# Pinning VectorE's order around the delta rule chain in a hybrid decoder step

## The chip, the cores and the metric

The kernel runs on one core of one Trainium2 chip, as one launch. The metric is the device time of that launch in microseconds (us). TensorE (PE) multiplies matrices, VectorE (DVE) and ScalarE (ACT) work element by element, GpSimd (POOL) does small things and issues transfers, and SyncE (SP) issues transfers. Each engine works through its own list of instructions; semaphores order the lists among each other.

## The reference

One decoder layer for 1024 prompt tokens and 8 sample tokens: a SwiGLU block, a mixer, a second SwiGLU block, each closed by a layer norm. The mixer runs an RG-LRU branch and a gated delta rule branch side by side. The change lies in the delta rule. For each of 8 heads and each chunk of tokens it computes, with a state S of 128 x 128:

```
def step(S, inp):
    qd, kt, ui, wi, ai, gl = inp
    v_new = ui - wi @ S
    o = qd @ S + ai @ v_new
    S = S * exp(gl) + kt.T @ v_new
    return S, o
...
o = o * rsqrt(mean(square(o), -1) + RMS_EPS) * gdn_norm_w
out_b = o * silu(z)
merged = sigmoid(gate_a) * out_a + sigmoid(gate_b) * out_b
return merged @ w_o
```

## The kernel before

All activations lie transposed, channels on the 128 partitions and the 1032 tokens along the free dimension, in three chunks of 344 (`TC`). Matmuls are done in three passes on operands split into a high and a low part (`mm3_steps`, L172). The kernel has three stages: the first SwiGLU up to some 740 us, the mixer up to some 1775 us, the second SwiGLU.

In the mixer two programs are woven together. The first is the delta rule of one head, the generator `gdn`: a preparation (norms, decays, the inverse of a triangular matrix), and then a chain of 8 chunks of 128 tokens. The second is the `stream`, the projections of the mixer's input with all that follows them: keys, queries and values of the next head, the RG-LRU (`rgx`, `rg`), the gates (`gate_b`, `gate_a`). Each `yield` of `gdn` names a weight from the table `W`; times a rate of some 2.1 it gives the number of steps of the stream (three matmuls each) that are issued before `gdn` goes on. The rate spreads the stream evenly over the heads.

The chain, per chunk c, in the program's order:
- p1 (from chunk 1 on): `K` and `Q` times the state `St` into a PSUM bank of the tag `sq` (two banks). VectorE makes r of it (L1103), ScalarE makes `to`. Then `yield W["s1"]`.
- p2: the inverse `U` times r. VectorE scales it by `cs` to v2 (L1110). Then `yield W["s2"]`.
- p3: `KT` and `AT` times v2. VectorE brings the state forward (`St`, L1115) and sums the chunk's output into `O`, which is the tile `vn` (L1116). ScalarE sums the output's squares into `os`. Then `yield W["s3"]`.

The generator `tail(j)` closes the outputs of half a head, four chunks. VectorE adds up (`os`), GpSimd takes the power -1/2 (`os<-os,NHALF`), and after a yield VectorE scales the outputs by these roots (L1087, `vn<-vn,os`, 128 x 512). Then TensorE transposes them (`trs`, L935) and VectorE multiplies them into the gate's tile `ACC`. The first half's tail starts at the end of chunk 3, its scaling stands in the program behind the output sum of chunk 4, and its rest comes after chunk 5. The second half's tail follows the last chunk.

Of the stream, one line matters below: `gate_b` closes each chunk of its projection with a VectorE multiply (L1143, `ACC<-lnq,ACC`) of ScalarE's tanh `lnq` with the gate. `rI<-rI,s` is an RG-LRU step (L1222), `s<-pre,conv_w,s` a step of a convolution (L801).

What sets the order: a compiler's list scheduler makes each engine's list ahead of time. By its own forecast of when operands are there, it takes of the instructions that are ready the earliest one of the program. `tc.keep_in_program_order(x)` (here `pin`) ties x behind the one instruction that the program gave x's engine just before it: x does not come ahead of that one in the list. It makes no semaphore and no wait for that one's end. In the chain the first matmul of each step is pinned in TensorE's list. The stream's matmuls are not, and on VectorE nothing in `gdn` is. Lines that are a helper's (L91 `act`, L94 `tt`, L97 `stt`, L929 `mms`) stand for many operations, so the rows below are read by their tiles.

Of the kernel before, what the change touches and what calls it, by code (L numbers as in the profile page):

```python
# [12 lines left out]
OP = mybir.AluOpType  # L13
# [46 lines left out]
def _build(ctx, tc, A):  # L60
    nc = tc.nc
    V, S, G, PE = nc.vector, nc.scalar, nc.gpsimd, nc.tensor
# [24 lines left out]
    def psum(tag):  # L87
        return ps.tile([128, 512], F32, name="ps_" + tag, tag=tag, bufs=PSB[tag])

    def act(out, in_, f, **kw):  # L90
        return S.activation(out, in_, f, **kw)  # L91

    def tt(out, a, b, op, eng=None):
        return (eng or V).tensor_tensor(out, a, b, op=op)  # L94

    def stt(out, a, s, b, op0, op1):
        return V.scalar_tensor_tensor(out, a, s, b, op0=op0, op1=op1)  # L97

    def bc(ap, shape):
        return ap.to_broadcast(shape)  # L100
# [579 lines left out]
    def mixer(mc):  # L680
# [74 lines left out]
        with pool("mix") as mp:  # L755
            B4 = [128, 4, 128]
# [10 lines left out]
            def blk(tag):  # L767
                return mp.tile([128, 128], F32, name=tag, tag=tag)

            def small(tag):  # L770
                return mp.tile([128, 8], F32, name=tag, tag=tag, bufs=2)
# [4 lines left out]
            def ck(x, c):  # L776
                return x[:, c * 128:(c + 1) * 128]
# [146 lines left out]
            def pin(ins):  # L924
                tc.keep_in_program_order(ins)

            def mms(p, pairs, pinned=True):
                for i, (a, b) in enumerate(pairs):
                    x = PE.matmul(ck(p, i), a, b, start=True, stop=True)  # L929
                    if i == 0 and pinned:  # L930
                        pin(x)

            def trs(p, ins):
                for i, a in enumerate(ins):
                    x = PE.transpose(ck(p, i), a, IDT)  # L935
                    if i == 0:
                        pin(x)

            def gdn(h):
                K, Q, v = KQV[h]  # L940
                C4 = [range(4 * j, 4 * j + 4) for j in range(2)]
                J = [slice(4 * j, 4 * j + 4) for j in range(2)]
                k2s, cs, nh, qe = small("k2s"), small("cs"), small("nh"), small("qe")
# [16 lines left out]
                for j in range(2):  # L960
                    pd = psum("g")
                    for i in range(2):
                        x = PE.matmul(pd, SLR, gu[j][i].rearrange("p c j -> p (c j)"), start=(i == 0), stop=(i == 1))
# [115 lines left out]
                O = VN  # L1079
                os_ = small("os")  # L1080

                def tail(j):
                    o = os_[:, J[j]]
                    stt(o, o, 1.0 / 128, qe[:, J[j]], OP.mult, OP.add)
                    tt(o, o, NHALF[:, :4], OP.pow, G)
                    yield W["ta"]
                    tt(O[:, J[j], :], O[:, J[j], :], bc(o.unsqueeze(2), B4), OP.mult)  # L1087
                    yield W["tb"]
                    yield ("need", ("B", h))
                    pt = psum("g")  # L1090
                    trs(pt, [O[:, c, :] for c in C4[j]])
                    js = slice(512 * j, 512 * j + 512)
                    stt(ACC[:, h, js], pt, NW, ZT[h][:, js], OP.mult, OP.mult)
                    yield W["tc"]

                St = blk("St")
                for c in range(CH):
                    r = VN[:, c, :]
                    if c > 0:
                        p1 = psum("sq")  # L1100
                        mms(p1, [(ck(K, c), St), (ck(Q, c), St)])
                        r = blk("r")
                        stt(r, p1[:, :128], NE[:, c, h:h + 1], VN[:, c, :], OP.mult, OP.add)  # L1103
                        to = blk("to")
                        act(to, p1[:, 128:256], AF.Copy, scale=EX[:, 0, c, h:h + 1])
                        yield W["s1"]
                    p2 = psum("sq")
                    mms(p2, [(U[:, c, :], r)])
                    v2 = blk("v2")
                    V.tensor_scalar(v2, p2[:, :128], cs[:, c:c + 1], None, op0=OP.mult)  # L1110
                    yield W["s2"]
                    p3 = psum("sq")
                    mms(p3, [(KT[:, c, :], v2), (AT[:, c, :], v2)])
                    if c > 0:
                        stt(St, St, EX[:, 2, c, h:h + 1], p3[:, :128], OP.mult, OP.add)  # L1115
                        tt(O[:, c, :], to, p3[:, 128:256], OP.add)  # L1116
                    else:
                        act(St, p3[:, :128], AF.Copy)
                        act(O[:, c, :], p3[:, 128:256], AF.Copy)
                    act(blk("jk"), O[:, c, :], AF.Square, accum_out=os_[:, c:c + 1])  # L1120
                    if c == 3:
                        t0 = tail(0)
                    if c in (3, 4):
                        next(t0)
                    yield W["s3"]
                    if c == 5:
                        yield from t0
                        done.add(("T", h))
                nc.scalar.dma_start(A["p_S"][h], St)
                yield from tail(1)  # L1130

            ZT = {}
# [178 lines left out]
            for h in range(H):  # L1311
                while ("K", h) not in done:
                    next(st)
                last = h == H - 1
                rate = units / H * (LAST if last else (H - LAST) / (H - 1)) / sum(w * COUNT.get(n, 1) for n, w in W.items())
                acc = 0.0
                for w in gdn(h):
                    if isinstance(w, tuple):
                        while w[1] not in done:
                            next(st)  # L1320
                        continue
                    acc += w * (WO_RATE if last and ("T", h) in done else rate)
                    while acc >= 1:
                        acc -= 1
                        next(st, None)
                done.add(("G", h))
                if ("A", h) in done and h < H - 1:
                    merge(h)
# [244 lines left out]
```

## Time and profile before

| | |
|---|---|
| median of 3 runs | 2529.0 us (2524.57 to 2530.25) |
| the profiled execution | 2523.32 us |
| its span, first to last instruction | 2521.5 us |
| TensorE busy | 2477.8 us, 98% |
| VectorE busy | 1825.7 us, 72% |
| ScalarE busy | 1178.4 us, 47% |
| mean granted TensorE clock | 0.993 |

All durations below are of the profiled execution. A row of a timeline gives the start from the span's beginning, the duration, the engine, the line, the operation, what it writes and reads, and in brackets how long the engine stood idle before it and what released it. Busy time of TensorE is modelled and includes the overlap of consecutive matmuls; a gap in it is real.

### The profile page before, as it was taken

The numbers are of one execution on the slowest core, as the hardware profiler recorded it, in microseconds if no ns is written. First come the engines' busy times: TensorE is split into PE (matmuls) and PEld (weight loads), VectorE is DVE, ScalarE is ACT, GpSimd is POOL, SyncE is SP. The second block draws the span as 40 slices with busy tenths as digits, with TensorE's granted clock in tenths as the row PEclk, the third lists the DMA queues.
The fourth block names the chain that finished last, engine by engine and source line by source line (L and its number), as shares of the span: only waits on it lengthen the run. The fifth ranks groups of instructions, "written<-read, shape, count | busy, mean of one in ns | idle before, by whom it ended". The sixth has DMA issues, their size and how long they took to land.

```text
span 2521.5 us, 48825 instructions
## 1 busy us (share of the span) xinstructions
PE 2477.8 (98%) x18758; PEld 2434.0 (97%) x18758; DVE 1825.7 (72%) x3967; ACT 1178.4 (47%) x2516; POOL 392.7 (16%) x663
## 2 busy tenths in 40 slices
PE   9999999999999999999999999999999999999997
PEld 8999999999998999999999999999899999999997
DVE  7777676687697677767777777767776777758876
ACT  5433333334353737364656555654553333333435
POOL 2122121001113022111111111120421111100010
PEclk9999999999998999999999999999999999999999
DMA  6566564868212021111111121234753545457653
GB/s 234 176 189 202 181 207 129 272 195 242 77 38 54 31 54 37 49 46 40 46 40 52 33 58 32 58 90 149 211 167 110 145 129 146 124 202 224 200 161 89
DMA packets 203561, 310.23 MB, mean 123 GB/s; under 512 B 41456, under 2 KB 85744, under 8 KB 203328
## 3 DMA queue, kind: packets, MB, share of 16 engines
q1 hardware_dynamic: 145760, 197.83, 25.4%
q0 software_dynamic: 46736, 103.22, 14.2%
q10 hardware_dynamic: 10832, 6.07, 0.9%
q8 instruction: 147, 2.41, 0.4%
q14 instruction: 86, 0.70, 0.1%
HBM read 231.35 MB, written 75.69 MB: 122 GB/s over the span
## 4 chain that ended last, share of the span: by engine, by line
PE 64%; issue 14%; DMA 6%; ACT 6%; DVE 6%; POOL 3%; SPq 0%; POOLq 0%; ACTq 0%; DVEq 0%
PE ps_mm L172 33%; PE ps_g L172 8%; PE ps_g L337 5%; PE ps_mm L337 5%; PE ps_sq L337 4%; DMA gr<-gt 3%; PE ps_g L1043 2%; ACT L91 2%; PE ps_sq L929 2%; POOL hv L142 1%; DVE ACC L97 1%; DVE wl L94 1%; PE ps_g L929 1%; PE ps_g L935 1%; ACT lnq L91 1%
## 5 line engine op out<-in xcount | busy, mean ns | idle before, releaser
L172 PE MATMUL ps_mm<-XH,wh 128*128 128x344 f32 (+1 forms) x2104 | 683.3, 325 | 5.7 <-ACT wh L91 5.5
L172 PE MATMUL ps_mm<-XL,wh 128*128 128x344 f32 (+1 forms) x2104 | 659.2, 313 | 0.0
L172 PE MATMUL ps_mm<-XH,wl 128*128 128x344 f32 (+1 forms) x2104 | 659.1, 313 | 0.0
L172 PEld LDWEIGHTS ps_mm<-XH,wh 128*128 128x128 f32 x2104 | 398.7, 190 | 9.0 <-ACT wh L91 5.5
L172 PEld LDWEIGHTS ps_mm<-XL,wh 128*128 128x128 f32 x2104 | 398.2, 189 | 1.4 <-DVE XL L94 0.5
L172 PEld LDWEIGHTS ps_mm<-XH,wl 128*128 128x128 f32 x2104 | 397.6, 189 | 0.4 <-DVE wl L94 0.2
L91 ACT ACTIVATE wh<-wraw 128x512 fp32r<-128x512 f32 (+1 forms) x346 | 212.0, 617 | 323.3 <-PE ps_mm L172 86.9
L94 DVE TENSOR_TENSOR wl<-wraw,wh 128x512 fp32r<-128x512 f32 (+1 forms) x346 | 232.3, 674 | 91.4 <-ACT wh L91 46.7
L337 PE MATMUL ps_g<-CH,wh 128*128 128x258 f32 x740 | 209.4, 283 | 1.3 <-DVE u L94 1.3
L337 PE MATMUL ps_g<-CH,wl 128*128 128x258 f32 x740 | 209.0, 282 | 0.0
L337 PE MATMUL ps_g<-CL,wh 128*128 128x258 f32 x740 | 208.7, 282 | 0.0
L172 PE MATMUL ps_g<-XH,wl 128*128 128x258 f32 (+1 forms) x592 | 175.1, 296 | 2.5 <-DVE wl L94 2.1
L172 PE MATMUL ps_g<-XH,wh 128*128 128x258 f32 (+1 forms) x592 | 173.3, 293 | 0.4 <-ACT wh L91 0.3
L172 PE MATMUL ps_g<-XL,wh 128*128 128x258 f32 (+1 forms) x592 | 172.9, 292 | 0.0
L337 PE MATMUL ps_mm<-XH,wl 128*128 128x258 f32 x592 | 167.6, 283 | 1.9 <-DVE wl L94 1.9
L337 PE MATMUL ps_mm<-XH,wh 128*128 128x258 f32 x592 | 167.2, 282 | 0.0
L337 PE MATMUL ps_mm<-XL,wh 128*128 128x258 f32 x592 | 166.8, 282 | 0.0
L91 ACT ACTIVATE wh<-S 128x512 fp32r<-128x512 f32 x148 | 92.9, 627 | 127.2 <-PE ps_sq L337 55.4
L91 ACT ACTIVATE XH<-gr 128x516 fp32r<-128x516 f32 x112 | 70.7, 635 | 170.2 <-DMA gr<-gt 161.3
L337 PEld LDWEIGHTS ps_g<-CH,wh 128*128 128x128 f32 x740 | 139.5, 189 | 1.9 <-DVE u L94 1.9
L91 ACT ACT_TABLE_LOAD x107 | 137.3, 1283 | 5.6 <-issue 2.6
L337 PEld LDWEIGHTS ps_g<-CL,wh 128*128 128x128 f32 x740 | 139.8, 189 | 0.0
(550 smaller groups left out, 6267.7 us busy)
## 6 DMA issues: line engine op xcount, KB each, us to landing
wraw<-w SPq DMA_DIRECT2D x212, 256.0 KB, 3.1
wraw<-w_in SPq DMA_DIRECT2D x128, 256.0 KB, 2.6
gt<-G POOLq DMA_DIRECT2D x112, 258.0 KB, 3.0
gr<-gt SPq DMA_DIRECT2D x112, 258.0 KB, 3.2
wr<-w SPq DMA_DIRECT2D x76, 256.0 KB, 3.4
hv<-wh POOLq DMA_DIRECT2D x42, 256.0 KB, 4.3
hv<-wl POOLq DMA_DIRECT2D x42, 256.0 KB, 4.4
wraw<-w_o SPq DMA_DIRECT2D x38, 256.0 KB, 3.0
```

The lines of the kernel that those rows point to most:

```text
L91: return S.activation(out, in_, f, **kw)
L94: return (eng or V).tensor_tensor(out, a, b, op=op)
L97: return V.scalar_tensor_tensor(out, a, s, b, op0=op0, op1=op1)
L142: G.dma_start(halves[key][i], x)
L172: PE.matmul(p, a, b, start=(n == 0), stop=(n == 3 * nk - 1))
L337: PE.matmul(ps_[c], a[:, k, :], b, start=(start and n == 0), stop=(n == 11), skip_group_check=not start)
L929: x = PE.matmul(ck(p, i), a, b, start=True, stop=True)
L935: x = PE.transpose(ck(p, i), a, IDT)
L1043: pin(PE.matmul(o[r, c, :], a(c), b(c), start=True, stop=True))
```

## The change

Two places of `gdn` get a pin: the scaling of the outputs by their roots (in both tails of every head), and the chain's scaling of v2 in chunks 3 to 7.

```
@@ -1084,7 +1084,7 @@
                     stt(o, o, 1.0 / 128, qe[:, J[j]], OP.mult, OP.add)
                     tt(o, o, NHALF[:, :4], OP.pow, G)
                     yield W["ta"]
-                    tt(O[:, J[j], :], O[:, J[j], :], bc(o.unsqueeze(2), B4), OP.mult)
+                    pin(tt(O[:, J[j], :], O[:, J[j], :], bc(o.unsqueeze(2), B4), OP.mult))
                     yield W["tb"]
                     yield ("need", ("B", h))
                     pt = psum("g")
@@ -1107,7 +1107,9 @@
                     p2 = psum("sq")
                     mms(p2, [(U[:, c, :], r)])
                     v2 = blk("v2")
-                    V.tensor_scalar(v2, p2[:, :128], cs[:, c:c + 1], None, op0=OP.mult)
+                    x = V.tensor_scalar(v2, p2[:, :128], cs[:, c:c + 1], None, op0=OP.mult)
+                    if c > 2:
+                        pin(x)
                     yield W["s2"]
                     p3 = psum("sq")
                     mms(p3, [(KT[:, c, :], v2), (AT[:, c, :], v2)])
```

The same instructions run with the same operands; only their places in VectorE's list, and what the scheduler makes of that, can differ.

## Rows read from the trace of the kernel before

**Rows 1.** The page, part 1: busy us (share of span) and instructions.

```profile
PE 2477.8 (98%) x18758; PEld 2434.0 (97%) x18758; DVE 1825.7 (72%) x3967; ACT 1178.4 (47%) x2516; POOL 392.7 (16%) x663
```

**Rows 2.** Busy time by stretch: stretch, its us, then busy us (instructions) of each engine.

```profile
990.00:1700.00 710.00, 704.76 (x5199) 685.20 (x5198) 515.39 (x1248) 398.25 (x918) 116.33 (x183) 1.00 0.17 49
```

**Rows 3.** TensorE's groups, 800 to 1700 us: busy, mean ns, idle before, releasers.

```profile
L929 PE MATMUL ps_sq<-v,kt 128*128 128x128 f32 x128 | 26.3, 287 | 5.9 <-ACT ACC L91 3.2 <-DVE s L97 1.3 <-DVE v L1110 0.7
...
L929 PE MATMUL ps_sq<-r,u 128*128 128x128 f32 x112 | 22.5, 283 | 2.3 <-DVE r L97 2.2
```

**Rows 4.** VectorE's group of the scalings, same columns.

```profile
L94 DVE TENSOR_TENSOR vn<-vn,os 128x512 f32<-128x512 f32 x16 | 11.1, 692 | 14.2 <-POOL os L94 14.2
```

**Rows 5.** VectorE's timeline, head 3: start us, us, instruction [idle before <-releaser].

```profile
1196.93 0.35 DVE L1110 TENSOR_SCALAR v<-ps_sq,cs 128x128 f32<-128x128 f32 x1 [0.22 <-PE ps_sq L929]
1198.32 0.35 DVE L97 SCALAR_TENSOR_TENSOR St<-St,EX,ps_sq 128x128 f32<-128x128 f32 x1 [1.04 <-PE ps_sq L929]
...
1200.18 0.35 DVE L97 SCALAR_TENSOR_TENSOR r<-ps_sq,NE,vn 128x128 f32<-128x128 f32 x1
1200.54 0.52 DVE L97 SCALAR_TENSOR_TENSOR ACC<-lnq,ACC 128x344 f32<-128x344 f32 x1
...
1202.43 0.69 DVE L94 TENSOR_TENSOR vn<-vn,os 128x512 f32<-128x512 f32 x1 [0.93 <-POOL os L94]
1203.39 0.52 DVE L97 SCALAR_TENSOR_TENSOR rI<-rI,s 128x344 f32<-128x344 f32 x1 [0.27 <-ACT rI L91]
1203.82 0.35 DVE L1110 TENSOR_SCALAR v<-ps_sq,cs 128x128 f32<-128x128 f32 x1
1204.09 0.56 DVE L97 SCALAR_TENSOR_TENSOR s<-pre,conv_w,s 128x336 f32<-128x336 f32 x1
...
1206.11 0.28 DVE L94 TENSOR_TENSOR vn<-to,ps_sq 128x128 f32<-128x128 f32 x1
```

**Rows 6.** TensorE's timeline, head 3, the chain's matmuls: p2, p3, p1, p3, p1, p2.

```profile
1196.51 0.38 PE L929 MATMUL ps_sq<-r,u 128*128 128x128 f32 x2
1197.67 0.38 PE L929 MATMUL ps_sq<-v,kt 128*128 128x128 f32 x2
...
1199.54 0.60 PE L929 MATMUL ps_sq<-St,ACC 128*128 128x128 f32 x4
...
1204.32 0.46 PE L929 MATMUL ps_sq<-v,kt 128*128 128x128 f32 x2 [0.64 <-ACT ACC L91]
...
1206.27 0.69 PE L929 MATMUL ps_sq<-St,ACC 128*128 128x128 f32 x4
1208.58 0.49 PE L929 MATMUL ps_sq<-r,u 128*128 128x128 f32 x2 [0.20 <-DVE r L97]
```

**Rows 7.** ScalarE's timeline, head 3: the gate's tanh, and that of `rI`.

```profile
1199.96 0.55 ACT L91 ACTIVATE lnq<-ps_mm,HBI 128x344 f32<-128x344 f32 x1
...
1202.82 0.54 ACT L91 ACTIVATE rI<-ps_g,HBR 128x344 f32<-128x344 f32 x1
```

**Rows 8.** Timeline of head 0: VectorE's r, straight behind the scaling, and TensorE's p2.

```profile
849.64 0.34 DVE L97 SCALAR_TENSOR_TENSOR r<-ps_sq,NE,vn 128x128 f32<-128x128 f32 x1
...
850.04 0.49 PE L929 MATMUL ps_sq<-r,u 128*128 128x128 f32 x2 [0.68 <-DVE r L97]
```

**Rows 9.** Timeline, 1294.5 to 1299.5: a GpSimd product, and VectorE's convolution steps beside it.

```profile
1295.59 1.05 POOL L94 TENSOR_TENSOR gu<-masks,GHL 128x512 fp32r<-128x512 f32 x1 [2.70 <-PE ps_g L1043]
...
1295.14 2.49 DVE L97 SCALAR_TENSOR_TENSOR s<-pre,conv_w,s 128x344 f32<-128x344 f32 x3
```

**Rows 10.** Head 7's end: VectorE and TensorE timeline; tile view (first to last start).

```profile
1702.32 0.69 DVE L94 TENSOR_TENSOR vn<-vn,os 128x512 f32<-128x512 f32 x1
...
1705.51 0.51 DVE L94 TENSOR_TENSOR s<-s,ACC 128x344 f32<-128x344 f32 x1
...
1704.80 0.60 PE L935 MATMUL ps_g<-masks,vn 128*128 128x128 f32 x4
...
L172 PE MATMUL ps_mm<-m_vn,wh x12: 317/321/421, 1727.2 to 1772.3; 128*128 128x344 f32 x12
```

More of the change, by code (lines that the diff above doesn't have):

```diff
@@ L1086, in tail @@
                     yield W["ta"]
-                    tt(O[:, J[j], :], O[:, J[j], :], bc(o.unsqueeze(2), B4), OP.mult)
+                    pin(tt(O[:, J[j], :], O[:, J[j], :], bc(o.unsqueeze(2), B4), OP.mult))
                     yield W["tb"]
@@ L1109, in gdn @@
                     v2 = blk("v2")
-                    V.tensor_scalar(v2, p2[:, :128], cs[:, c:c + 1], None, op0=OP.mult)
+                    x = V.tensor_scalar(v2, p2[:, :128], cs[:, c:c + 1], None, op0=OP.mult)
+                    if c > 2:
+                        pin(x)
                     yield W["s2"]
```

## The prediction

> **What bounds the kernel now.** I read the page's busy line first. TensorE is busy 98% of the span, VectorE 72% [rows 1]. So a VectorE instruction has a price only where TensorE waits for it. Next I took the stage in which the change lies, the mixer's heads: from 990 to 1700 us TensorE is busy 704.76 of 710 us [rows 2], so some 5 us can be won there altogether. Third, the TensorE groups of the heads by what they idled for: before p3 (`ps_sq<-v,kt`) 5.9 us, before p2 (`ps_sq<-r,u`) 2.3 us, in 128 and 112 records [rows 3]. These 8.2 us are nearly all that the delta rule chain costs TensorE, and they bound a gain from above: 0.3%.
>
> Fourth, VectorE's own view of the scaling: 16 of them, 692 ns each, with 14.2 us of idle time in front, all of it waiting for GpSimd's root [rows 4]. VectorE works through its list in order, so that wait holds everything behind it. This is the waste that the eye finds, but it is VectorE's time and not TensorE's; the timeline must say what stood behind it.
>
> Fifth, one head in full (head 3; heads 2 to 6 repeat it, and the 3.2 us that [rows 3] put down to ScalarE are its 0.64 us gap five times). Around the scaling VectorE's order is: v2 of chunk 3 at 1196.93, r of chunk 4 at 1200.18, the gate's closing multiply (`ACC<-lnq,ACC`) at 1200.54, the scaling at 1202.43 after 0.93 us of waiting, `rI` at 1203.39 after another 0.27 us of waiting for ScalarE, v2 of chunk 4 at 1203.82, the output sum of chunk 4 at 1206.11 [rows 5]. TensorE has one large gap there, 0.64 us before p3 of chunk 4 at 1204.32, and 0.20 us before p2 of chunk 5 [rows 6]. The trace puts the first down to ScalarE; p3 reads v2, and it starts 0.15 us after v2's end (1203.82 + 0.35 = 1204.17), so I take v2 as the cause.
>
> **Which instructions the change moves.** A pin ties an instruction to the one instruction that the program gave VectorE just before it, and nothing more. So I followed the program's generators and compared each pinned instruction's predecessor with VectorE's order in the trace.
> - The first half's scaling (8 of them): the predecessor is the output sum of chunk 4. In the trace the scaling runs ahead of that sum in all eight heads; in head 3 by 3.7 us [rows 5]. All eight move behind it.
> - The second half's scaling: in heads 1 to 6 the predecessor has long run. In head 0 it changes places with its neighbour. In head 7 it must wait for the layer norm's sum at 1705.51 and now runs at 1702.32 [rows 10].
> - v2 of chunks 3 to 7 (40 of them): in 35 cases the predecessor is r of the same chunk or something that has already run, and the pin changes nothing. The five others are chunk 3 of heads 2 to 6: while the chain yields between p1 and p2, the stream gives VectorE the gate's closing multiply, which waits for ScalarE's tanh, and v2 ran ahead of it. In head 3 that multiply comes at 1200.54, 3.6 us after v2 [rows 5], as soon as the tanh (1199.96 + 0.55 = 1200.51) is there [rows 7].
>
> No instruction is added or removed, and no transfer moves of itself; all costs are waits.
>
> **The first half's scaling.** Taken out of its place it frees 0.93 us of waiting and 0.69 us of work. In head 0 exactly this stands before r of chunk 4: the scaling ends, r starts at 849.64, and TensorE has waited 0.68 us when p2 starts at 850.04 [rows 8]. That gap goes: -0.7 us. In heads 2 to 6 I do not credit it with the 0.64 us. Behind the scaling stands `rI`, and that waits for ScalarE (1202.82 + 0.54 = 1203.36 [rows 7]) whether the scaling is there or not; v2 would still start at 1203.82. Where it goes, behind the sum of chunk 4, the root is long finished, and its reader, the transposes after chunk 5, comes a chunk later: nothing on the path. If that cover were gone, it would cost its own 0.69 us in a head.
>
> **v2 of chunk 3.** It cannot start before the multiply. r no longer stands ahead of that, so the multiply still starts at 1200.54; the next instruction follows such a one 0.43 us later (1203.39 to 1203.82 [rows 5]), so v2 starts at 1200.97 instead of 1196.93: 4.0 us later. What is queued behind it on VectorE is stream work without haste. Who waits is p3 (0.50 us after v2's start, as in chunk 4): 1201.47 instead of 1197.67 [rows 6], 3.8 us later. Two bounds for the price:
> - Upper: TensorE's order stays as it is and it stands idle, 3.8 us less the 0.64 us gap that then lies inside the same shift, so 3.2 us in each of five heads: +16 us.
> - Lower: TensorE's order is made by the same rule as VectorE's, the earliest of what is ready; only the first matmul of each step of the chain is pinned, and the projections' matmuls are not. They may go ahead of p3. Then TensorE does other work in these 3.8 us and nothing is lost.
>
> I take the lower one. The shift is also soon made up, by the chain's own latencies: p3 at 1201.47, St 0.65 later (1197.67 to 1198.32), p1 0.50 after it, r 0.64 later (1199.54 to 1200.18), p2 0.50 later, v2 0.42 later (1196.51 to 1196.93), p3 0.50 later. That sums to 1204.68 for p3 of chunk 4, against 1204.32 now; p1 of chunk 5 could start at 1204.68 + 0.65 + 0.50 = 1205.83, and its place is at 1206.27 [rows 5, 6]. So one chunk is enough, with 0.4 us in hand.
>
> On the way, though, four steps (p3, p1, p2 and p3 again) run with no slack, and the compiled order rests on forecast times that are now and then a few tenths off: the 0.20 us and 0.64 us gaps are of that kind. From below: both gaps go, -0.84 us a head, -4.2 us in five. From above: a gap of 0.2 to 0.64 us at each of four steps, 0.8 to 2.6 us a head, less the 0.84 us: up to +8.8 us. The nearest row is the present pattern, one 0.64 and one 0.20 in a head, now at other steps, so I take 0.
>
> **The second half's scaling in head 7.** From 1702.32 to about 1705.95, 3.6 us later. Its readers are transposes, the last merge and the splits of the output projection's operand; that projection reads the last of these from 1727.2 on [rows 10], and 17 us of cover is enough. The transposes, now at 1704.80, could hold TensorE for up to 1.8 us (1705.95 + 0.69 - 1704.80) if nothing goes ahead of them; I take 0, since the projection's matmuls are free to.
>
> **Sum.** -0.7 (head 0) + 0 (heads 2 to 6) + 0 (head 7) = -0.7 us: 2523.3 - 0.7 = 2522.6 against the profiled execution (2521.5 us of span and 1.8 us around it). That one is 5.7 us below the median of the runs, 2529.0, so the forecast as a median is 2528. A measurement of this kernel can tell about 0.2%, 5 us, from no change; this is no change.
>
> **Rivals.**
> 1. Clean win. What VectorE gains in front of the scaling reaches TensorE in every head: the shifted chain puts v2 of chunk 4 behind `rI` at no cost, and no step of the compiled order is left tight. Then both gaps of heads 2 to 6 go: -4.2 - 0.7 = -4.9 us, 2524. For it: all these gaps lie in the reordered stretch. Against it: ScalarE's lateness, which stands behind v2 of chunk 4, is not touched. 0.15. The Trainium skill (PSUM — Partial Sum Buffer, Engine vs sequencer instructions) says that VectorE's queue is strictly first in, first out, by which a wait taken from its middle brings forward all that stands behind it; the trace agrees in head 0 (r starts as the scaling ends), and by that rule alone this rival would be the forecast.
> 2. TensorE keeps its order, and stands before p3 of chunk 3: +16 us, 2545, slower. It decides from the point where no unpinned matmul is ready when p1's turn has passed. For it: in this stretch TensorE's list follows the program almost word for word. Against it: the next projection chunk has its operands and weights. 0.10.
> 3. Tight chain: small gaps at each of the four steps, +4 to +9 us, 2533 to 2538, on the edge of slower. 0.17.
> 4. The root no longer runs beside an idle VectorE but beside the convolutions. Three of their steps beside a GpSimd product took 2.49 us, 0.83 each, where one alone has 0.56 [rows 9, 5]. At 3 x 0.27 = 0.8 us of VectorE a head, all of it on the chain, that is 6 us: 2534. The Trainium skill (SBUF — State Buffer, Who interferes with whom) has it that a VectorE instruction with two SBUF inputs and a GpSimd instruction that reads SBUF lock each other out. The product's row agrees; the root has only 4 columns. 0.05.
>
> The change not doing what it says lies in the forecast already: 35 of 40 pins on v2 hold by themselves.
>
> **How the numbers follow.** Forecast 0.53, rivals 0.15, 0.10, 0.17 and 0.05. Faster by over 0.2%: half of rival 1, which lies on that edge, and the low end of the forecast, 0.13. Slower: rival 2, two thirds of 3 and 4 (0.15), 0.25. Same: the rest, 0.62. The range takes the forecast's own (2523 to 2533, the scatter of the runs) and extends to rivals 1 and 3 and 4, leaving out 2: 2520 to 2537.
>
> **What would show it.** Right: TensorE's busy time in the heads within 5 us of now; the scalings without idle time before them; p2 of head 0 at 850 without its gap; in heads 2 to 6, v2 of chunk 3 straight behind the gate's multiply, some 3.5 to 4 us later against p2 than now, with projection matmuls between p2 and p3 instead of a gap. Wrong: a gap of 1 us or more before p3 of chunk 3 (rival 2), new gaps before p1 and p2 of chunk 4 (3), or none at all in the heads (1).

## The result: slower by 0.6%, with a ratio of 1.0064

The changed kernel takes 2544.2 us (median of 8 runs, 2531.43 to 2549.26), the kernel before, beside it on the same chip, 2525.91 us (8 runs). The ratio is 1.0064, with a 95% interval of 1.0048 to 1.008: 12 to 20 us slower. The forecast was 2528 with a range up to 2537; the time lies above it. The profiled execution of the changed kernel took 2543.21 us, its span is 2541.4 us, its mean granted clock 0.991.

The page's busy line of the changed kernel, to be laid beside [rows 1]:

```profile
PE 2483.9 (98%) x18758; PEld 2437.3 (96%) x18758; DVE 1827.8 (72%) x3967; ACT 1185.7 (47%) x2521; POOL 392.1 (15%) x663
```

Span less TensorE's busy time was 2521.5 - 2477.8 = 43.7 us and is now 2541.4 - 2483.9 = 57.5: of 19.9 us more of span, 13.8 are idle TensorE. The other 6.1 are TensorE busy for longer with the same 18758 matmuls. (This is one execution of each; the medians are 18.3 us apart.)

Where is that? The tile view of `os` gives the first and the last of 16 root sums, one for each half of a head, and so the length of the heads without anything ahead of them or behind (minimum, median and maximum ns, then first to last start). The changed kernel, then the kernel before:

```profile
L97 DVE SCALAR_TENSOR_TENSOR os<-os,qe x16: 155/158/166, 845.5 to 1704.0; 128x4 f32<-128x4 f32 x16
```

```profile
L97 DVE SCALAR_TENSOR_TENSOR os<-os,qe x16: 154/157/164, 847.8 to 1700.8; 128x4 f32<-128x4 f32 x16
```

The heads have grown from 853.0 to 858.5 us, by 5.5; the rest of the span behind them from 820.7 to 837.4, by 16.7; ahead of them it is 2.3 us less. So there are two losses, and the larger one lies behind the stage in which nearly all of the change stands.

**In the heads.** TensorE's groups of the chain, 845 to 1710 us, in the columns of [rows 3]: p3, p2, and the two forms of p1.

```profile
L929 PE MATMUL ps_sq<-v,kt 128*128 128x128 f32 x120 | 25.2, 292 | 3.9 <-DVE v L1110 2.5 <-DVE s L97 1.3
L929 PE MATMUL ps_sq<-r,u 128*128 128x128 f32 x106 | 21.2, 281 | 4.1 <-DVE r L97 4.1
...
L929 PE MATMUL ps_sq<-St,ACC 128*128 128x128 f32 x98 | 15.9, 279 | 1.3 <-DVE St L97 1.3
L929 PE MATMUL ps_sq<-St,kq 128*128 128x128 f32 x100 | 15.8, 280 | 2.0 <-DVE St L97 2.0
```

The idle time before p3 fell from 5.9 to 3.9 us, but before p2 it rose to 4.1 (1.8 in the same stretch of the kernel before), and before p1, where there was none, there are 3.3. That is 11.3 us after 7.7, 3.6 of the 5.5 us by which the heads have grown. The scalings themselves did what the change says; their group, which answers to [rows 4]:

```profile
L94 DVE TENSOR_TENSOR vn<-vn,os 128x512 f32<-128x512 f32 x16 | 11.0, 688 | 5.4 <-POOL os L94 5.4
```

Their idle time fell from 14.2 to 5.4 us. VectorE won 8.8 us, and TensorE lost time. Head 3 shows how. VectorE's timeline, which answers to [rows 5]:

```profile
1200.01 0.51 DVE L97 SCALAR_TENSOR_TENSOR ACC<-lnq,ACC 128x344 f32<-128x344 f32 x1
1200.44 0.34 DVE L1110 TENSOR_SCALAR v<-ps_sq,cs 128x128 f32<-128x128 f32 x1
1201.74 0.52 DVE L97 SCALAR_TENSOR_TENSOR rI<-rI,s 128x344 f32<-128x344 f32 x1 [0.95 <-ACT rI L91]
...
1202.65 0.34 DVE L97 SCALAR_TENSOR_TENSOR St<-St,EX,ps_sq 128x128 f32<-128x128 f32 x1
...
1219.55 0.52 DVE L94 TENSOR_TENSOR rI<-rI,lnq 128x344 f32<-128x344 f32 x1 [0.62 <-ACT lnq L91]
1219.98 0.34 DVE L97 SCALAR_TENSOR_TENSOR r<-ps_sq,NE,vn 128x128 f32<-128x128 f32 x1
1220.24 0.91 DVE L1226 TENSOR_TENSOR_SCAN ga<-rR,HL,rI 128x336 f32<-128x336 f32 x1
...
1221.13 0.68 DVE L94 TENSOR_TENSOR wl<-wraw,wh 128x512 fp32r<-128x512 f32 x1
1221.73 0.34 DVE L1110 TENSOR_SCALAR v<-ps_sq,cs 128x128 f32<-128x128 f32 x1
```

And TensorE's timeline, which answers to [rows 6]: p2 and p3 of chunk 3, p1 of chunk 4, p2 and p3 of chunk 6.

```profile
1195.40 0.38 PE L929 MATMUL ps_sq<-r,u 128*128 128x128 f32 x2
...
1200.93 0.46 PE L929 MATMUL ps_sq<-v,kt 128*128 128x128 f32 x2
...
1203.05 0.71 PE L929 MATMUL ps_sq<-St,ACC 128*128 128x128 f32 x4 [0.65 <-DVE St L97]
...
1220.38 0.49 PE L929 MATMUL ps_sq<-r,u 128*128 128x128 f32 x2 [0.64 <-DVE r L97]
...
1222.22 0.46 PE L929 MATMUL ps_sq<-v,kt 128*128 128x128 f32 x2 [0.40 <-DVE v L1110]
```

v2 of chunk 3 stands straight behind the gate's multiply, and p3 follows it without a gap: TensorE did projection matmuls from p2 at 1195.40 to p3 at 1200.93. But now the state's update `St` stands behind `rI`, which waited 0.95 us for ScalarE, and p1 of chunk 4 comes 0.65 us late. The 0.64 us of [rows 6] are not gone, they have changed their step. In chunk 6, where no pin acts, r stands behind the product `rI<-rI,lnq`, which waited 0.62 us for ScalarE's square root, and v2 behind a scan and a split of weights: 0.64 and 0.40 us that the kernel before did not have. From the first half's scaling in head 2 (1084.86) to that in head 3 (1206.79) it is now 121.93 us, and was 1202.43 - 1081.59 = 120.84: 1.09 us more a head, of which these three gaps (1.69 us) less the 0.64 and 0.20 of [rows 6] are 0.85.

What is it that VectorE waits for? ScalarE's timeline ahead of that square root:

```profile
1216.75 0.96 ACT L91 ACTIVATE lnq<-ps_mm,HBI 128x344 f32<-128x344 f32 x2
1217.73 1.28 ACT L91 ACT_TABLE_LOAD   x1
1219.03 0.49 ACT L91 ACTIVATE lnq<-lnq 128x344 f32<-128x344 f32 x1
```

ScalarE worked without a pause, and 1.28 us of that were the loading of the root's table. The RG-LRU step asks for a sigmoid, an exponential and a square root in turn. That became theory T below.

**Behind the heads.** Behind the last root sum TensorE is idle for 28.2 us where it was for 20.4: 7.8 of the 16.7 us. The other 8.9 are longer busy time of the same matmuls. In the trace the clock lies at the lower of its two levels, half speed, for 33.1 us of that stretch, in the kernel before for 17.0; inside the heads it does so in neither. As an estimate from these figures, 16.1 us more at half speed are some 8 us. So in these two executions waits and clock share the loss about equally.

From 1700 to 1860 us TensorE was busy 154.59 us of 160 at a granted clock of 0.98; now it is 149.11 at 0.95. What it waited for at the output projection, 1780 to 1860 us (waiter, releaser, total us, times, longest):

```profile
PE ps_g L172 <- DMA wl<-hv: 1.8, 2, 1.5
PE ps_g L172 <- DMA wh<-hv: 1.6, 2, 1.0
PE ps_mm L172 <- DMA wl<-hv: 0.6, 1, 0.6
```

And in the kernel before:

```profile
PE ps_g L172 <- DMA wl<-hv: 0.3, 1, 0.3
```

That is 4.0 us of waiting for fetches of the output weights (`wh`, `wl`, from the scratch `hv`), where the same stage of the kernel before had 0.3. These fetches are issued by GpSimd. GpSimd's timeline of the changed kernel:

```profile
1810.64 0.55 POOL L269 DMA_DIRECT2D x<-ACC  x1 [9.63 <-ACT ACC L91]
1811.18 0.55 POOL L150 DMA_DIRECT2D wh<-hv  x1
```

A store of the layer norm's result (`x<-ACC`, L269) waits 9.63 us for ScalarE, and the next fetch stands behind it. TensorE's matmul on that fetch starts at 1816.59 after 0.95 us of waiting. In the kernel before the fetches are issued from 1789.65 to 1811.04 with no store between them, and the next store comes only at 1811.70:

```profile
1811.04 0.53 POOL L150 DMA_DIRECT2D wh<-hv  x1 [0.83 <-PE ps_mm L172]
1811.70 0.55 POOL L269 DMA_DIRECT2D x<-ACC  x1
```

That became theory C.

### The profile page after: what moved, and what is told of

Read it like the earlier page. It is cut to its first block, busy times and chain, and to the rows that moved or that the text cites. A ratio compares the mean times of both kernels' runs of the same rounds, so it can differ in the third digit from the quotient of the medians.

```text
span 2541.4 us, 48821 instructions
## 1 busy us (share of the span) xinstructions
PE 2483.9 (98%) x18758; PEld 2437.3 (96%) x18758; DVE 1827.8 (72%) x3967; ACT 1185.7 (47%) x2521; POOL 392.1 (15%) x663
## 4 chain that ended last, share of the span: by engine, by line
PE 66%; issue 12%; ACT 7%; DMA 6%; DVE 5%; POOL 3%; POOLq 0%; SPq 0%; DVEq 0%; ACTq 0%
PE ps_mm L172 32%; PE ps_g L172 8%; PE ps_g L337 6%; PE ps_mm L337 6%; PE ps_sq L337 5%; DMA gr<-gt 3%; ACT L91 3%; PE ps_g L1043 2%; PE ps_sq L929 2%; POOL hv L142 1%; ACT lnq L91 1%; PE ps_g L929 1%; DVE wl L94 1%; PE ps_g L935 1%; DVE XL L94 1%
```

## The experiments

Unless the text says otherwise, a kernel is the one before with the edit named; e1 to e14 are the numbers of the kernels. "At full clock" is each run's time multiplied by its mean granted clock, averaged over the runs; it is worked out, and takes TensorE as busy throughout; the clock stands there to 0.001, which is 2.5 us of one run. The clocks of the runs beside the changed kernel are not on record, so its 2522.7 us at full clock are set against the 2511.1 to 2512.1 of the four sets of runs beside the experiments. The heads' length is that of the root sums, as above, in the one profiled execution of each kernel.

| kernel | median us (runs) | kernel before beside it | ratio (95%) | at full clock, less before | heads, us |
|---|---|---|---|---|---|
| before | | 2526 to 2530 | | 0 | 853.0 |
| changed | 2544.2 (8) | 2525.91 | 1.0064 (1.0048 to 1.008) | +10.5 to +11.6 | 858.5 |
| e1, all scalings | 2548.64 (6) | 2527.86 | 1.0086 (1.0056 to 1.0116) | +16.1 | 859.8 |
| e2, v2 alone | 2537.23 (12) | 2527.86 | 1.0034 (1.0016 to 1.0052) | +7.0 | 857.1 |
| e3, all but head 7's last scaling | 2534.79 (12) | 2527.86 | 1.0025 (1.0006 to 1.0045) | +5.7 | 858.3 |
| e4, head 7's last scaling alone | 2539.11 (12) | 2527.86 | 1.0047 (1.0029 to 1.0065) | +7.1 | 852.8 |
| e5, before, no table in the recurrence | 2531.17 (1) | 2526.11 | | | 845.9 |
| e6, changed, no table in the recurrence | 2528.2 (1) | 2526.11 | | | 842.3 |
| e7, `rI` held instead | 2538.61 (6) | 2526.11 | 1.0042 (1.003 to 1.0055) | +8.6 | 860.8 |
| e8, changed, `rI` held too | 2552.83 (1) | 2526.11 | | | 861.2 |
| e9, before, one table fewer | 2522.62 (12) | 2529.91 | 0.9967 (0.9954 to 0.998) | -7.0 | 848.0 |
| e10, changed, one table fewer | 2532.45 (12) | 2529.91 | 1.0007 (0.9993 to 1.0021) | -4.5 | 846.3 |
| e11, before, stores by SyncE | 2526.83 (12) | 2529.91 | 0.9997 (0.9983 to 1.0011) | -1.2 | 853.0 |
| e12, e4 with stores by SyncE | 2529.22 (12) | 2529.91 | 0.9996 (0.9979 to 1.0012) | -0.5 | 852.9 |
| e13, before, both | 2522.98 (12) | 2529.02 | 0.9979 (0.9964 to 0.9995) | -7.8 | 848.6 |
| e14, changed, both | 2527.01 (12) | 2529.02 | 0.9986 (0.9971 to 1.0001) | -7.9 | 846.1 |

By this column some 11 of the changed kernel's 18.3 us are left at full clock. The rest goes with the granted clock and the scatter of the runs.

### Which part costs what: e1 to e4

Theory A: two parts cost, v2 of chunk 3 in the heads and head 7's last scaling behind them. Theory B: the stage behind the heads suffers from the late chains of heads 2 to 6.

e1, the scalings alone, which does what the first hunk of the change does:

```
-                    tt(O[:, J[j], :], O[:, J[j], :], bc(o.unsqueeze(2), B4), OP.mult)
+                    x = tt(O[:, J[j], :], O[:, J[j], :], bc(o.unsqueeze(2), B4), OP.mult)
+                    if True:
+                        pin(x)
```

> Only the scalings by the roots are pinned, both halves, in all heads; v2 is as before. Theory A (the heads lose some 5 us through v2 of chunk 3, the stage behind them some 13 us through the second half's scaling of head 7): heads (990 to 1700) as before within 1 us, the stretch behind them some 13 us longer, +12 us in all. Theory B (the stage behind the heads suffers because the chains of heads 2 to 6 arrive late): no change, 0 to -1 us.

e2, v2 alone (the second hunk):

```
-                    V.tensor_scalar(v2, p2[:, :128], cs[:, c:c + 1], None, op0=OP.mult)
+                    x = V.tensor_scalar(v2, p2[:, :128], cs[:, c:c + 1], None, op0=OP.mult)
+                    if c > 2:
+                        pin(x)
```

> Only v2 is pinned, in chunks 3 to 7. Theory A: +5 us, all of it in heads 2 to 6, as gaps before p1, p2 and p3 of the chunks after chunk 3, about 1 us a head; nothing behind the heads. Theory B: +17 us, 5 in the heads and 12 behind them.

e3, the changed kernel without the pin on the last scaling of head 7:

```
-                    pin(tt(O[:, J[j], :], O[:, J[j], :], bc(o.unsqueeze(2), B4), OP.mult))
+                    x = tt(O[:, J[j], :], O[:, J[j], :], bc(o.unsqueeze(2), B4), OP.mult)
+                    if (h, j) != (7, 1):
+                        pin(x)
```

> The whole change, but the second half's scaling of head 7 stays without a pin. Theory A: +5 us, with the stage behind the heads as before. Theory B: +17 us as with the whole change.

e4, that pin alone (`if (h, j) == (7, 1)`, and nothing on v2):

> One pin alone, on the second half's scaling of head 7. Theory A: +13 us, none of it before 1695 us. Theory B: no change.

Measured: +20.8, +9.4, +6.9 and +11.3 us by the medians. e4 leaves the heads as they were, 852.8 us, and costs 11.3 us; every engine's list is that of the kernel before up to 1702 us, so the cost comes from what lies behind. e2 and e3 lengthen the heads by 4.1 and 5.3 us. e3 and e4 together (18.2) give the whole change (18.3). So head 7's pin costs its 11 us without any late chain, as theory A says and B does not, and e3, with late chains and without that pin, costs 6.9.

e2 fits A less well. It was to cost 5 us and nothing behind the heads; it cost 9.4, of which 4.1 lie in the heads. In its trace the stretch behind them is 828.0 us long, after 820.7, though there no engine's list differs from that of the kernel before; in e7 and e9, again with the same lists there, it is 830.9 and 829.5. So one trace leaves some 7 to 10 us of that stretch open, and whether late chains lengthen it (theory B as a smaller part) is not shown.

e1 is a miss in the heads. It was to leave them unchanged and cost 12 us; they are the longest of the four, +6.8 us, and it costs 20.8, more than the whole change. The first half's scalings are not free. TensorE, and VectorE ahead of its second gap, in head 3 of e1:

```profile
1207.90 0.46 PE L929 MATMUL ps_sq<-v,kt 128*128 128x128 f32 x2 [0.64 <-ACT ACC L91]
1224.64 0.49 PE L929 MATMUL ps_sq<-r,u 128*128 128x128 f32 x2 [0.46 <-DVE r L97]
1227.35 0.46 PE L929 MATMUL ps_sq<-v,kt 128*128 128x128 f32 x2 [1.11 <-DVE v L1112]
```

```profile
1225.37 0.92 DVE L1226 TENSOR_TENSOR_SCAN ga<-rR,HL,rI 128x336 f32<-128x336 f32 x1
...
1226.86 0.35 DVE L1112 TENSOR_SCALAR v<-ps_sq,cs 128x128 f32<-128x128 f32 x1
```

The 0.64 us of [rows 6] are still there, and in chunk 6, two chunks behind the moved scaling, v2 now stands behind the scan, where in the kernel before it ran at 1222.05, ahead of the scan at 1222.32. A moved instruction changes what the scheduler finds ready from there on, so the list differs where nothing was pinned. It follows too that the parts don't add up in the heads: 6.8 and 4.1 us alone, 5.5 together.

### Why the heads lose: e5 to e10

Theory T: what costs is that a step of the chain stands behind an instruction that waits for ScalarE, and ScalarE is late by its table loads. Rival U: the order alone costs, whatever ScalarE does. In e5 (before) and e6 (changed) ScalarE loads no table in the heads:

```
-                    act(R, pr, AF.Sigmoid, bias=RGT[:, 1, c:c + 1])
+                    act(R, pr, AF.Tanh, bias=RGT[:, 1, c:c + 1])
-                    act(R, R, AF.Exp, scale=NSP8[:, 0, c:c + 1])
+                    act(R, R, AF.Tanh, scale=NSP8[:, 0, c:c + 1])
-                    act(M, M, AF.Sqrt, scale=0.25)
+                    act(M, M, AF.Tanh, scale=0.25)
```

> The kernel before, with the recurrence's three kinds of activation that ask ScalarE for other tables (Sigmoid, Exp, Sqrt) all replaced by Tanh, so that ScalarE loads no table inside the heads; the recurrence's values are thereby other ones and its output is not the reference's. To be read beside the next kernel, which is the changed one with the same edit. Theory T (the time in the heads comes from chain steps that stand on VectorE behind an instruction of the recurrence, which waits for a ScalarE that is late by its table loads of 1.28 us): the gaps of about 1 us a head that TensorE has in the kernel before (0.64 ahead of p3 of chunk 4, 0.20 and 0.13 ahead of p2 of chunk 5) shrink, and the pitch of heads 2 to 6 falls from 120.84 to 119.9 to 120.3 us. Rival U (the gaps come from TensorE's and VectorE's order alone, whatever ScalarE does): gaps and pitch stay at 120.8 or move by the order without a pattern.

> The changed kernel with the same edit (Sigmoid, Exp and Sqrt of the recurrence replaced by Tanh; its output is not the reference's). Theory T: without the late ScalarE the changed order of VectorE costs nothing in the heads, the gaps of 0.65 (p1 of chunk 4), 0.64 and 0.40 (p2 and p3 of chunk 6) go below 0.2, and the pitch of heads 2 to 6 falls from 121.93 to within 0.3 us of the kernel before with the same edit. Rival U: the pitch stays about 1 us above that of the kernel before with the same edit. Behind the heads both say that the change still costs 5 to 13 us, since that part comes from the last scaling.

ScalarE's table loads in the changed kernel, and in e6:

```profile
L91 ACT ACT_TABLE_LOAD x112 | 143.7, 1283 | 5.5 <-issue 2.6 <-DVE ga L1226 1.0
```

```profile
L91 ACT ACT_TABLE_LOAD x19 | 24.4, 1283 | 2.9 <-issue 2.6
```

TensorE's groups p3 and p2 in e6, 845 to 1710 us:

```profile
L929 PE MATMUL ps_sq<-v,kt 128*128 128x128 f32 x120 | 23.6, 278 | 0.1
L929 PE MATMUL ps_sq<-r,u 128*128 128x128 f32 x105 | 21.3, 283 | 0.0
```

And the heads, e5 first:

```profile
L97 DVE SCALAR_TENSOR_TENSOR os<-os,qe x16: 154/158/165, 851.3 to 1697.2; 128x4 f32<-128x4 f32 x16
```

```profile
L97 DVE SCALAR_TENSOR_TENSOR os<-os,qe x16: 153/156/164, 842.1 to 1684.4; 128x4 f32<-128x4 f32 x16
```

The chain's gaps are gone, 0.1 us where the changed kernel had 11.3. The heads take 845.9 us in e5 and 842.3 in e6; from one of heads 2 to 6 to the next (the pitch) it is 119.56 and 118.99 us. So with ScalarE in time the change shortens the heads by 3.6 us, further than theory T was put. Only 0.7 us of that is idle TensorE (1.8 us in e5, 1.1 in e6); where the rest comes from was not followed.

There is a catch. Without the table loads the scheduler makes other lists: from the kernel before to e5 some 300 of VectorE's instructions change places in the heads, where the change itself moves some 120. So these two runs take away the lateness and change the order as well, and by themselves don't shut out rival U. One pair that stayed together speaks for T: in e6 `rI` still stands straight ahead of v2 of chunk 4 in head 3, as in [rows 5], and neither waits.

```profile
1192.88 0.51 DVE L97 SCALAR_TENSOR_TENSOR rI<-rI,s 128x344 f32<-128x344 f32 x1
1193.31 0.34 DVE L1110 TENSOR_SCALAR v<-ps_sq,cs 128x128 f32<-128x128 f32 x1
```

(One run each, 2531.17 and 2528.2 us; the heads are read from the traces.)

If T is right, can the wait be pinned out of the way? e7 holds `rI`, the instruction that stands ahead of v2 of chunk 4, in the kernel before, and e8 does so in the changed one:

```
-                    stt(I, I, 1.0, XC, OP.add, OP.mult)
+                    pin(stt(I, I, 1.0, XC, OP.add, OP.mult))
```

> The kernel before, with one more instruction of the recurrence held to the program's order on VectorE, the product (rI+1) times xc, which in the kernel before stands ahead of v2 of chunk 4 and waits for ScalarE; nothing of the change is in it. Theory T: v2 of chunk 4 no longer waits behind it, the 0.64 us ahead of p3 of chunk 4 goes in each of heads 2 to 6, the pitch falls from 120.84 to 120.2 to 120.4, and the kernel is 2 to 4 us faster than before, ratio 0.9985 to 0.999. Rival: another step of the chain comes to stand behind another instruction that waits, as with the change itself: pitch 120.8 to 121.9, time 0 to 6 us more.

> The changed kernel with the same product of the recurrence held to the program's order. Theory T: the gap of 0.65 us ahead of p1 of chunk 4 goes, since the state's update no longer stands behind that product; the 0.64 and 0.40 us ahead of p2 and p3 of chunk 6 stay, since these stand behind another instruction (the product with the square root): pitch of heads 2 to 6 121.2 to 121.4 after 121.93. Rival: the held product moves the list elsewhere and the pitch stays at 121.9 or more.

Both fell to the rival. e7 costs 12.5 us with none of the change in it, twice what even the rival allowed; 7.8 us lie in the heads, where the pitch is 122.0 us, and the rest was not traced. TensorE's gaps in head 3 of e7:

```profile
1203.77 0.46 PE L929 MATMUL ps_sq<-v,kt 128*128 128x128 f32 x2 [0.27 <-DVE v L1110]
1208.35 0.49 PE L929 MATMUL ps_sq<-r,u 128*128 128x128 f32 x2 [0.61 <-DVE r L97]
1221.27 0.49 PE L929 MATMUL ps_sq<-r,u 128*128 128x128 f32 x2 [0.73 <-DVE r L97]
1223.53 0.46 PE L929 MATMUL ps_sq<-v,kt 128*128 128x128 f32 x2 [0.35 <-DVE v L1110]
```

The 0.64 became 0.27, the 0.20 ahead of p2 of chunk 5 became 0.61, and two came in chunk 6: 1.96 us in all, after 0.84. In e8 the gap before p1 of chunk 4 went, and one of 0.81 us came before its p3, with v2 behind a root sum that waited 1.42 us for ScalarE; from head 2's first scaling to head 3's it is 122.04 us (1093.86 to 1215.90). In these two, with ScalarE late, the pin only chose which step stood behind it.

So the other end: make ScalarE less late. e9 (before) and e10 (changed) write the sigmoid as (tanh(x/2)+1)/2, with the half and the one folded into the scale and bias of its readers; the result stays the reference's.

```
+        HBA = mc.tile([128, KD], F32, name="HBA")
...
+            act(HBA, RGT[:, 1, :], AF.Copy, scale=0.5)
...
-            act(SP8, NSP8, AF.Copy, scale=8.0)
-            act(NSP8, NSP8, AF.Copy, scale=-8.0)
+            act(SP8, NSP8, AF.Copy, scale=4.0)
+            act(NSP8, NSP8, AF.Copy, scale=-4.0)
...
-                    act(R, pr, AF.Sigmoid, bias=RGT[:, 1, c:c + 1])
+                    act(R, pr, AF.Tanh, scale=0.5, bias=HBA[:, c:c + 1])
                     act(I, pi, AF.Tanh, scale=0.5, bias=HBR[:, c:c + 1])
-                    act(Tt, R, AF.Tanh, scale=SP8[:, 0, c:c + 1])
-                    act(R, R, AF.Exp, scale=NSP8[:, 0, c:c + 1])
+                    act(Tt, R, AF.Tanh, scale=SP8[:, 0, c:c + 1], bias=SP8[:, 0, c:c + 1])
+                    act(R, R, AF.Exp, scale=NSP8[:, 0, c:c + 1], bias=NSP8[:, 0, c:c + 1])
```

> The kernel before with the recurrence's Sigmoid written as (tanh(x/2)+1)/2, the half and the one folded into the scale and bias of the two activations that read it, so that the output stays the reference's and ScalarE needs one table fewer a third (two loads of 1.28 us where the kernel before has three, some 24 fewer in all if tanh and exp then stand in one table). Theory T (the heads' gaps come from a ScalarE that is late by its table loads): part of the gaps of about 1 us a head goes, pitch of heads 2 to 6 119.6 to 120.6 us after 120.84, time 2 to 8 us less than before. Rival U (gaps come from the order alone): pitch 120.8 or more, time within 3 us of before.

> The changed kernel with the same rewriting of the recurrence's Sigmoid (output as the reference's). Theory T: with fewer table loads the change costs the heads less than the 4.8 us that it cost before, its pitch within 0.5 us of that of the kernel before with the same rewriting or below it; behind the heads it still costs what head 7's last scaling costs, 5 to 13 us, so it stays slower than the kernel before with the rewriting by 4 to 12 us. Rival U: the pitch stays 1 us above, the whole difference 12 to 20 us as measured.

Table loads of e9:

```profile
L91 ACT ACT_TABLE_LOAD x67 | 86.0, 1283 | 3.8 <-issue 2.6
```

67 after 107 in the kernel before. The Trainium skill (ScalarE: Activation LUTs, Table sets: the hidden batching unit) has tanh in the table set of exp as well as in that of sigmoid; the fall agrees. e9 is 7.3 us faster than the kernel before (0.9967), a version that beats both; its pitch is 120.05 us. In e10 the pitch is 119.74 and the heads are 1.7 us shorter than in e9, and still it is 9.8 us slower: none of that lies in the heads. At full clock 2.5 us of it are left (-4.5 against -7.0); the other 7 go with the clock, 0.9904 in the mean of e10's runs and 0.9932 in e9's. In both pairs the change is a gain in the heads once ScalarE is less late, which is what theory T says: its lateness turns this gain into a loss. That the lists are other ones too stays a reservation.

### Why the stage behind the heads loses: e11 to e14

Theory C: a store that waits stands ahead of the fetches in GpSimd's list. Rival D: TensorE's clock and other orders. e11 (before) and e12 (e4) issue the stores from SyncE:

```
-                    G.dma_start(X2[:, k, self.s], y)
+                    nc.sync.dma_start(X2[:, k, self.s], y)
```

> The kernel before with the stores of x2 to memory issued by SyncE in place of GpSimd; nothing of the change is in it. It is the comparison for the next kernel. Theory C (in the changed kernel GpSimd's list puts a store of x2, which waits 8.2 us for ScalarE, ahead of the fetches of the output projection's weights, and TensorE then waits for these): before has the fetches in time, so moving the stores does little here, within 3 us of before. Rival: the stores' place on SyncE's queue delays the state loads there, 3 to 10 us more.

> Head 7's last scaling alone held to the order, as in the run that cost 11.9 us, with the stores of x2 issued by SyncE. Theory C: the fetches of the output weights no longer stand behind a store that waits, the gaps of 1.1 to 1.5 us ahead of matmuls on these weights go, and the held scaling costs 0 to 5 us against the kernel before with the same stores. Rival D (the cost behind the heads is TensorE's granted clock and other orders, not these fetches): it stays 9 to 14 us slower than the kernel before.

TensorE's waits for the fetches from 1780 to 1860 us, in e4 and then in e12:

```profile
PE ps_g L172 <- DMA wh<-hv: 3.1, 3, 1.3
...
PE ps_g L172 <- DMA wl<-hv: 1.1, 1, 1.1
```

```profile
PE ps_g L172 <- DMA wh<-hv: 0.4, 1, 0.4
```

4.2 us became 0.4, and the held scaling costs 2.4 us (2529.22 against 2526.83) where it had cost 11.3; at full clock 0.7 after 7.1. TensorE's list is the same in e4 and e12 from first to last, VectorE's up to 1858 us, so the "other orders" of rival D are out: theory C holds. In e4 the store waits 8.23 us, in the whole change 9.63. Moving the stores does nothing by itself (e11).

The waits that went are 3.8 us, and the cost fell by 8.9. The clock has a part in the difference: e4's 12 runs have 0.9917 in the mean, those of the kernel before beside them 0.9933, which is 4 of the 11 us. With the stores moved it is 0.9926 and 0.9932. That the waits bring the clock down is not shown.

e13 and e14 have both edits, the sigmoid and the stores:

> The kernel before with both causes taken away: the recurrence's Sigmoid written with tanh (fewer table loads) and the stores of x2 issued by SyncE. It is the comparison for the next kernel: 4 to 10 us faster than the kernel before, as with the rewriting alone, since moving the stores did nothing alone; pitch of heads 2 to 6 120.0 us.

> The changed kernel with both causes taken away. If the two are the whole cost (theory T and theory C together): pitch of heads 2 to 6 119.6 to 120.1 us, no gaps ahead of the fetches of the output weights, time within 3 us of the kernel before with both, thus 4 to 12 us faster than the kernel before. Rival E (a third part): 4 us or more slower than the kernel before with both.

At full clock they are nearly equal, -7.8 and -7.9 us; by the ratios they are 0.0007 apart (some 2 us), by the medians 4.0 us, by the means of the 12 runs 1.2 us (2524.6 and 2525.8). The pitches, 120.05 and 119.76 us, are as expected, and of the waits for fetches one of 1.3 us is left in e14. So the two causes carry the 18.3 us but for a rest of 0 to 4 us that these runs can't settle: with the medians 4.0 us apart, rival E is not shut out. Nor is e14 faster than the kernel before by the 4 to 12 us expected; it is 2.0 by the medians, and its interval reaches 1.0001.

## Why the prediction was wrong

**What held.** The forecast was 2528 us within 2520 to 2537; 2544.2 is outside. In the mechanism this much was right. All first halves' scalings moved, and stand without idle time before them; those of heads 1 to 6 in the second half did not change (5.4 us, six times 0.9). v2 of chunk 3 starts 0.43 us after the gate's multiply, to the hundredth what was put, and p3 comes 5.53 us after p2 (1.16 before), some 4.4 us later where 3.8 was put. TensorE's list went round it: no gap, so the lower bound of that term was right and rival 2's mechanism did not occur, though its 2545 is nearly the time measured; that is chance. Rival 4 did not show: the root's median is 1037 ns, in the kernel before 1186. (Of the three steps of [rows 9] only the one that overlapped with the product is longer, 1.27 us; the other two took 0.58 each.) The busy time in the heads stayed within 5 us of before (700.76 against 704.76, 990 to 1700 us).

**Head 0, -0.7 us: did not come.** The scaling left, and r came no earlier with regard to its matmul. VectorE and TensorE in head 0, to be laid beside [rows 8]:

```profile
847.14 0.52 DVE L97 SCALAR_TENSOR_TENSOR rI<-rI,s 128x344 f32<-128x344 f32 x1 [1.49 <-ACT rI L91]
847.58 0.34 DVE L97 SCALAR_TENSOR_TENSOR r<-ps_sq,NE,vn 128x128 f32<-128x128 f32 x1
...
847.98 0.49 PE L929 MATMUL ps_sq<-r,u 128*128 128x128 f32 x2 [0.89 <-DVE r L97]
```

The next wait in the list took the scaling's place: `rI`, for ScalarE, and the gap is 0.89 us after 0.68. For heads 2 to 6 the prediction had reasoned just so, for head 0 not.

**The tight steps of heads 2 to 6, put at 0 with bounds of -4.2 and +8.8: +5.5 us.** The bounds held, the value in them was wrong. The prediction let the chain run on at its latencies, St 0.65 us after p3 and p1 0.50 after St, and asked of each step only when its operand is there. (The rows give 0.40 from r to p2, [rows 8], and in the changed kernel 0.40 from St to p1, where 0.50 was put; this changes nothing.) In the trace St comes 1.72 us after p3, since `rI` stands ahead of it. The prediction had named that wait, 0.27 us in the kernel before, and placed it before v2 alone. Shift the chain by 4 us and the wait falls on another step; the total was then settled by where the scheduler put the steps in chunk 4 and again in chunk 6. "One chunk is enough" was right for the chain's operands and wrong for the list, which stays different. This is rival 3 at its lower end, with one more place.

**Head 7's last scaling, put at 0 behind 17 us of cover: +11 us** (e4). The step looked at VectorE, the transposes and the projection's matmuls, and as far as it went it was right: against the last root sum the scaling comes 3.2 us later (3.6 put), and TensorE waits 0.6 us for it ahead of the transposes (up to 1.8 put). It did not follow the pin into the lists that issue transfers, and had said that "no transfer moves of itself". With the scaling held, the scheduler put stores and fetches into another order on GpSimd, and a fetch came to stand behind a store with 9.63 us of waiting. The term was not mis-sized, its place was missing. A lower clock came on top (e4), for which the sum had no term; why it fell is open.

The range ended at 2537, since head 7's term had 1.8 us as its upper end and the rivals, each of at most 9 us apart from rival 2, stood as alternatives that are not added. The two losses do add up: 5.5 us (heads, one trace) and 11.3 (e4, medians) are the 18.3 measured, to 1.5 us.

## What to carry to other kernels

Where a scheduler makes the lists, the price of holding one instruction can lie less in its own delay than in what the steps of the tight chain come to stand behind, in every engine's list from there to the end, the queues of transfers included. Ask which engine is late (here ScalarE, by its tables) and take away its lateness, rather than choosing by pins which step pays for it. And give loads that TensorE will need another queue than stores that wait for a late result.

## What the runs showed of the hardware that was not expected

A switch of tables costs the load and next to nothing else: the activation before it ends at 1216.75 + 0.96 = 1217.71, the root starts at 1219.03, 1.32 us for a load of 1.28; over all 122 switches of the changed kernel the median of this distance is 1.31 us. The Trainium skill (ScalarE: Activation LUTs, What ACT_TABLE_LOAD costs) adds a drain of about 1.38 us, 2.66 us in all; here the trace decides for 1.32.

The granted clock is part of the time behind the heads, but no single stretch of it shows a price. Windows of the changed kernel and then of the one before, 1755 to 1772 us (columns as in [rows 2], the clock third from the end):

```profile
1755.00:1772.00 17.00, 15.62 (x71) 15.31 (x70) 5.88 (x13) 1.95 (x7) 0.00 (x0) 0.60 0.43 131
```

```profile
1755.00:1772.00 17.00, 16.55 (x112) 15.52 (x111) 8.95 (x27) 4.08 (x13) 0.55 (x1) 1.00 0.51 151
```

A mean of 0.60 is mostly the lower of the two levels (1.2 GHz), and 41 matmuls fewer were done. Just ahead of it and at its start TensorE did matmuls of 2 columns (L1416) and waited 0.37 and 1.01 us for state loads. That this brought the clock down is argued, not shown. And the same window has 0.60 in e12, which costs 2.4 us, and 0.90 in e4, which costs 11.3. Over the runs about half of the scatter goes with the clock: in 35 runs of the kernel before, 2521.3 to 2540.43 us, the correlation between time and clock is -0.73.
